# A chunked recurrence that takes all its heads through each step together

## The chip, the cores and the metric

The kernel runs on one core of a Trainium2 chip, as one launch. The metric is the time of one execution on the device in microseconds (us), shorter being better. A core has a matrix engine (TensorE: PE in the profile, with PEld for its weight loads), a vector engine (DVE), a scalar engine (ACT), GpSimd (POOL) and SyncE (SP), which here issues most of the DMAs. Each engine works through its own instructions in their order. Matrix results land in PSUM, from where DVE or ACT carries them to SBUF.

## The reference

Two layers over 2048 tokens of width 1024, 16 heads of 64. Layer 0 is RWKV-7 time mixing, layer 1 a dilated sliding-window attention. This document is about layer 0, whose recurrence is, per head and token:

```python
def step(state, inp):
    r_t, w_t, k_t, v_t, a_t, b_t = inp
    sa = jnp.einsum('bhvk,bhk->bhv', state, a_t)
    state = (state * w_t[:, :, None, :]
             + sa[..., None] * b_t[:, :, None, :]
             + v_t[..., None] * k_t[:, :, None, :])
    return state, jnp.einsum('bhvk,bhk->bhv', state, r_t)
...
y = _wkv7_scan(r, decay, k, v, -kk, kk * a)
y = ((y - mu) * lax.rsqrt(var + GN_EPS)).reshape(B, S, D) * ln_g + ln_b
bonus = jnp.sum(r * k * r_k, axis=-1, keepdims=True) * v
y = (y + bonus.reshape(B, S, D)) * jax.nn.silu(g)
return y @ w_out
```

## The kernel before

`phase1` makes the projections, `phase2` runs the recurrence and the output projection of layer 0, `phase3` is layer 1. All arithmetic is float32; a large matmul is three matmuls of split halves (`mm3`, L72 to L74).

In `phase2` the 2048 tokens are 32 chunks of 64. The state is carried from chunk to chunk, so each chunk depends on the one ahead of it. A chunk's work has these parts:

- **Loads** (`loads`, L844 to L866, on SP): the receptance and removal keys `ls1`, the keys `bk`, inverted blocks `tf`, corrections `ut` and the values in `x`, for the next chunk. `ls1`, `tf` and `ut` have two buffers, `bk` has one.
- **Preparation** (`prep`, L869 to L915) of the next chunk, which needs no state: products of keys (L881, tile `z`, 8 matmuls for each half of the heads), masked or copied out of PSUM by ACT (`ot`, L885) and DVE (L886, L888), small 32x32 products (L894, L903), and transposes of the keys (L910), which are the last to read `bk`.
- **The chain** (`chain`, L930 to L981), in three dependent steps. Step 1 multiplies the state `x` by the removal keys into `ps` (L942) and by the receptance into `y` (L944); `evac` copies the first half of `ps` to `qc` on ACT and the second on DVE, one behind the other. Step 2 applies the inverted blocks (L959), and the result is copied over the state's rows in `x` (L927 on ACT, then L928 on DVE). Step 3 makes the next state's update in `ps` (L965) and the rest of the output in `y` (L967); DVE scales it (`up`, L973) and adds the decayed state `xp` (L976), which POOL made from `x` in step 1 (L955).
- **The rest of the layer**, one chunk or more behind: group norm (`group_norm`, on DVE, ACT and POOL), transposes of the finished output (`finish`, L1024) and the output projection (`out_proj`, matmuls into `pd`, 128x128 weights); in the first chunks also the tail of phase 1's gate projection.

The heads are taken in two halves, `a` (heads of blocks 0 to 3) and `b` (blocks 4 to 7). Each half has its own pass through the three steps, half `b` about half a chunk behind half `a`, and its last step stands in the next chunk's turn (`behind`). Each turn of a half is followed by a slot, in which every other part gets one step:

```python
a, b = (chain(ch, hb, ls, yc) for hb in range(2))
for i, g in enumerate((a, behind, a, behind, a, b, a, b, a, b)):
    next(g, None)
    ...
    slot(i, ch)
```

That is the order in which the program records the work; the framework's scheduler then moves instructions on each engine by its own timeline. It is held by a few ties: an output projection's matmuls may not stand ahead of the chain's mark `LAG` steps back (`spread`, with `marks`), and some DVE work not ahead of the copy `DLAG` copies back (`yielding`, with `dmarks`).

Of the kernel before, what the change touches and what calls it, by code (L numbers as in the profile page):

```python
# [37 lines left out]
RATE = (2.4, 2.05)  # L38
# [10 lines left out]
class Trunk:  # L49
# [747 lines left out]
    def phase2(self, keep):  # L797
        tc, nc, ap = self.tc, self.nc, self.ap
        mm = nc.tensor.matmul
# [3 lines left out]
        with ExitStack() as ctx:  # L803
            def pool(name, bufs, ctx=ctx, **kw):
                return ctx.enter_context(tc.tile_pool(name=name, bufs=bufs, **kw))
            cctx = ExitStack()
            np_, xp, yp, zp, sp = pool("np", 1, keep), pool("xp", 3, keep), pool("yp", 2, keep), pool("zp", 3, keep), pool("sp", 4, keep)
            gp, tp = pool("gp", 2, keep), pool("tp", 2, keep)
            pz = pool("pz", 2, keep, space=PSUM)
            self.kept = dict(xp=xp, yp=yp, zp=zp, gp=gp, tp=tp, pz=pz)  # L810
            bp, ep, lp, kp = pool("bp", 1, cctx), pool("ep", 1, cctx), pool("lp", 2, cctx), pool("kp", 1, cctx)
            pc, py = pool("pc", 2, cctx, space=PSUM), pool("py", 2, cctx, space=PSUM)
            late = {}

# [4 lines left out]
            rows = (slice(0, 64), slice(64, 128))  # L819
            ls1, tf, ut = [], [], []  # L820
            for i in range(2):
# [5 lines left out]
                for s in range(2):  # L827
                    pmark = nc.gpsimd.memset(t[64 * s + 32:64 * s + 64, :, 0:32], 0.0)
# [97 lines left out]
            def evac(dst, src):  # L926
                nc.scalar.activation(dst[0], src[0], AF.Copy)  # L927
                dmarks.append(nc.vector.tensor_copy(dst[1], src[1]))  # L928

            def chain(ch, hb, ls2, yc):  # L930
                nonlocal pmark
                b, xt = ch % 2, X[ch]
                h = slice(4 * hb, 4 * hb + 4)
                hd = [(s, 4 * hb + j) for j in range(4) for s in range(2)]
                if ch == 0:
                    for s in range(2):
                        nc.vector.memset(xt[rows[s], s, h], 0.0)
                ps = pc.tile([P, 2, 4, 64], F32, name="ps")
                y = py.tile([P, 4, 64], F32, name="y")
                first = [None, None]  # L940
                for s, j in hd:
                    mm(ps[rows[s], 0, j - 4 * hb], ls1[b][:, s, j, 0], xt[:, s, j], start=True, stop=True)  # L942
                for s, j in hd:
                    i = mm(y[rows[s], j - 4 * hb], ls1[b][:, s, j, 1], xt[:, s, j], start=first[s] is None,  # L944
                           stop=False, skip_group_check=True)
# [5 lines left out]
                xp_ = kp.tile([P, 4, 64], F32, name="xp%d" % hb)  # L951
                pc_ = self.pch[:, ch // 4, ch % 4, h].unsqueeze(2).to_broadcast([P, 4, 64])
# [5 lines left out]
                for s, j in hd:  # L958
                    i = mm(ps[rows[s], 1, j - 4 * hb], tf[b][rows[s], j], qc[rows[s], j - 4 * hb], start=True, stop=True)  # L959
                marks.append(i)  # L960
                evac([xt[rows[s], s, h] for s in range(2)], [ps[rows[s], 1] for s in range(2)])
                yield
                if ch < NCH - 1:
                    for s, j in hd:
                        mm(ps[rows[s], 0, j - 4 * hb], ls2[:, s, j, 1], xt[:, s, j], start=True, stop=True)  # L965
                for s, j in hd:
                    i = mm(y[rows[s], j - 4 * hb], ls2[:, s, j, 0], xt[:, s, j], start=False, stop=True, skip_group_check=True)  # L967
                marks.append(i)
                if ch < NCH - 1:
                    nxt = [X[ch + 1][rows[s], s, h] for s in range(2)]  # L970
                    if ch:
                        up_ = kp.tile([P, 4, 64], F32, name="up")
                        nc.vector.tensor_tensor(up_, ps[:, 0], pc_, op=ALU.mult)  # L973
                    for s in range(2):
                        if ch:
                            nc.vector.tensor_tensor(nxt[s], up_[rows[s]], xp_[rows[s]], op=ALU.add)  # L976
                        else:
                            nc.vector.tensor_tensor(nxt[s], ps[rows[s], 0], pc_[rows[s]], op=ALU.mult)
                yield
                nc.scalar.activation(yc[:, h], y, AF.Copy)  # L980
                yield  # L981

            def group_norm(ch, yc, zc):
# [138 lines left out]
            for _ in prep(0, bks, ls2):  # L1122
                pass
            idle = iter(())
            gn, pre, behind = idle, idle, idle
            zs = []

            def slot(i, ch):
                nonlocal tail
                next(pre, None)  # L1130
                next(gn, None)
                next(elim, None)
                now[0] += 1
                if tail:
                    for _ in range(TAIL[i % 2]):
                        if tail and next(tail, 1) == 1:
                            tail = None
                fill(1, front)
                fill(2 if len(work) > 1 and ch >= RUSH else 1)
# [8 lines left out]
            for ch in range(NCH):  # L1148
                ls = ls2
                pre = idle  # L1150
                if ch + 1 < NCH:
                    bks = loads(ch + 1)
                    ls2 = lp.tile([P, 2, KC, 2, 64], F32, name="ls2")
                    pre = prep(ch + 1, bks, ls2)
                yc = yp.tile([P, KC, 64], F32, name="yc")
                a, b = (chain(ch, hb, ls, yc) for hb in range(2))
                for i, g in enumerate((a, behind, a, behind, a, b, a, b, a, b)):
                    next(g, None)
                    if i == 3 and ch:
# [6 lines left out]
                behind, ylast = b, yc  # L1166
            for _ in behind:
                pass
# [649 lines left out]
```

## Time and profile before

| | |
|---|---|
| median of 3 runs | 3888.3 us (3877.28 to 3890.25) |
| profiled execution | 3889.0 us |
| its span on the core | 3887.1 us |
| the recurrence: first matmul of step 1 to last of step 3 | 1086.4 to 1839.0 us, 752.6 us |
| one chunk, 752.6 / 32 | 23.5 us |
| TensorE busy in the whole span | 3700.6 us, 95% |

The profile is of one execution. Its own time is 0.7 us above the median. Starts are in us from the span's start. A row's busy time on PE runs from a matmul's start to its modelled end, and matmuls overlap, so the pace of matmuls is read from the distance of starts. A float32 matmul of the recurrence leaves two records in the trace: "x16" there is 8 matmuls. The transposes (L910, L1024) and the projections' split matmuls leave one each. The granted clock of PE (PEclk) is 1.0 at 2.4 GHz and 0.5 at 1.2 GHz.

### The profile page before, as it was taken

To read this page: it belongs to the slowest core of one execution; us is meant where nothing else is said; L and a number is where in the kernel's file an instruction comes from. 1 tells how busy PE (TensorE), PEld (TensorE's weight loads), DVE (VectorE), ACT (ScalarE), POOL (GpSimd) and SP (SyncE) were. 2 spreads that over 40 slices of the span, in tenths; PEclk is the share of its full clock that TensorE was granted. 3 is DMA by queue.
4 is the path that set the end of the run, shared out by engine and by line. 5 is a ranking of instruction groups with operands and counts; after the bars stand their busy time and mean duration, and the time that the engine had idled before them with its cause. 6 is when DMAs were issued, how large, how long until landed. Compare 5 with 4: busy or idle time off the path is not lost.

```text
span 3887.1 us, 79932 instructions
## 1 busy us (share of the span) xinstructions
PE 3700.6 (95%) x29328; PEld 2930.5 (75%) x29328; DVE 2494.7 (64%) x6213; ACT 1822.1 (47%) x4734; POOL 1430.8 (37%) x1377
## 2 busy tenths in 40 slices
PE   7899999999989999999898999999999999999999
PEld 5565667767777888888776877777777788887888
DVE  4884477889866565465576347777876664455556
ACT  4554443343334443344444233456666665565441
POOL 3341355564344343333344234533432220023232
PEclk9899999999979998899999999999999999999999
DMA  9774467675665443343578455665655565456655
GB/s 279 224 242 138 131 181 205 175 211 163 175 134 124 99 111 90 89 109 92 135 124 167 138 160 79 118 144 144 183 149 136 134 171 138 148 168 193 188 165 174
DMA packets 1027128, 595.31 MB, mean 153 GB/s; under 512 B 564912, under 2 KB 918576, under 8 KB 1020592
## 3 DMA queue, kind: packets, MB, share of 16 engines
q1 hardware_dynamic: 629040, 500.00, 46.1%
q10 hardware_dynamic: 397696, 90.20, 11.1%
q8 instruction: 232, 3.80, 0.4%
q14 instruction: 160, 1.31, 0.1%
HBM read 391.84 MB, written 198.18 MB: 152 GB/s over the span
## 4 chain that ended last, share of the span: by engine, by line
PE 69%; DVE 12%; DMA 7%; issue 4%; POOL 4%; ACT 2%; SPq 1%; ACTq 0%; DVEq 0%; POOLq 0%
PE ps L72 12%; PE ps L74 11%; PE ps L73 11%; PE sc L1640 4%; PE z L881 4%; PE pv L1672 4%; PE z L1661 3%; PE pd L72 2%; PE pd L73 2%; DVE q L1215 2%; PE pd L74 1%; POOL rr_st L1207 1%; DMA bk<-bkD 1%; PE z L269 1%; PE ps L942 1%
## 5 line engine op out<-in xcount | busy, mean ns | idle before, releaser
L1652 ACT ACTIVATE yt<-yt,nm 128x256 f32<-128x256 f32 (+1 forms) x768 | 345.1, 450 | 294.6 <-DVE nm L1648 293.8
L72 PE MATMUL ps<-xh,wh 128*128 128x512 f32 (+1 forms) x1248 | 449.7, 369 | 7.2 <-ACT xh L358 5.6
L73 PE MATMUL ps<-xl,wh 128*128 128x512 f32 (+1 forms) x1248 | 448.0, 360 | 5.4 <-DVE xl L360 4.0
L74 PE MATMUL ps<-xh,wl 128*128 128x512 f32 (+1 forms) x1248 | 445.1, 358 | 0.0
L72 PE MATMUL ps<-xh 128*128 128x512 f32 (+1 forms) x1152 | 419.1, 364 | 4.3 <-ACT ov L1485 2.8
L74 PE MATMUL ps<-xh,xl 128*128 128x512 f32 (+1 forms) x1152 | 400.4, 348 | 0.0
L73 PE MATMUL ps<-xl,xh 128*128 128x512 f32 (+1 forms) x1152 | 398.5, 346 | 0.0
L1207 POOL TENSOR_TENSOR rr_st<-rr_st,mh 128x8 f32<-128x8 f32 x128 | 215.6, 1684 | 469.6 <-DVE rr_st L1206 411.4
L74 PE MATMUL ps<-wh,xl 128*128 128x512 f32 x896 | 362.8, 407 | 14.4 <-DVE xl L66 13.8
L72 PE MATMUL ps<-wh,xh 128*128 128x512 f32 x896 | 370.8, 415 | 4.8 <-ACT q L1450 1.7
L73 PE MATMUL ps<-wl,xh 128*128 128x512 f32 x896 | 361.2, 403 | 0.7 <-DVE wl L1286 0.6
L72 PEld LDWEIGHTS ps<-xh,wh 128*128 128x128 f32 x1248 | 238.9, 193 | 81.3 <-issue 35.8
L1645 DVE CUSTOM_DVE_ANT_0 yt<-sc,amask 128x256 f32<-128x256 f32 (+1 forms) x768 | 237.2, 360 | 86.6 <-PE sc L1640 80.5
L73 PEld LDWEIGHTS ps<-xl,wh 128*128 128x128 f32 x1248 | 240.3, 193 | 60.7 <-issue 18.2
L74 PEld LDWEIGHTS ps<-xh,wl 128*128 128x128 f32 x1248 | 240.4, 193 | 51.6 <-issue 22.2
L72 PEld LDWEIGHTS ps<-xh 128*128 128x128 f32 x1152 | 218.0, 189 | 50.9 <-issue 19.0
L74 PEld LDWEIGHTS ps<-xh,xl 128*128 128x128 f32 x1152 | 217.8, 189 | 27.7 <-issue 0.3
L73 PEld LDWEIGHTS ps<-xl,xh 128*128 128x128 f32 x1152 | 218.5, 190 | 23.0 <-issue 0.3
L1212 POOL TENSOR_TENSOR rr_a<-rr_sq,TCS 128x512 f32<-128x512 f32 x128 | 183.4, 1433 | 114.4 <-DVE rr_sq L1210 98.0
L278 DVE SCALAR_TENSOR_TENSOR t<-hx,vecs,t 128x512 f32<-128x512 f32 x192 | 170.5, 908 | 81.9 <-ACT t L277 81.6
L1215 DVE TENSOR_TENSOR q<-rr_sq,TCS 128x256 f32<-128x256 f32 x256 | 219.7, 898 | 2.6
L74 PEld LDWEIGHTS ps<-wh,xl 128*128 128x128 f32 x896 | 172.0, 192 | 63.9 <-DVE xl L66 26.3
(341 smaller groups left out, 8830.7 us busy)
## 6 DMA issues: line engine op xcount, KB each, us to landing
hx<-hT SPq DMA_DIRECT2D x152, 256.5 KB
xb<-xbT SPq DMA_DIRECT2D x256, 128.0 KB
x<-Q SPq DMA_DIRECT2D x96, 256.0 KB
kq<-K SPq DMA_DIRECT2D x72, 256.0 KB
st<-in_w_in SPq DMA_DIRECT2D x64, 256.0 KB
arD<-ar SPq DMA_DIRECT2D x32, 512.0 KB
bkD<-bk SPq DMA_DIRECT2D x32, 512.0 KB
ls<-arD SPq DMA_DIRECT2D x64, 256.0 KB
```

The lines of the kernel that those rows point to most:

```text
L72: i = mm(out, lh, rh, start=first, stop=False, **kw)
L73: mm(out, lh, rl, start=False, stop=False, **kw)
L74: mm(out, ll, rh, start=False, stop=last, **kw)
L278: nc.vector.scalar_tensor_tensor(t1, hx[:, 0:512], self.vec["a_mix_mu"][:, m:m + 1], t1, op0=ALU.mult, op1=ALU.add)
L881: mm(at[s][:, j], bk[rows[s], 4 * hb + j].rearrange("p a t -> p (a t)"), ls1[b][rows[s], s, 4 * hb + j].rearrange("p a t -> p (a t)"), sta ...
L1207: nc.gpsimd.tensor_tensor(st[:, 1], st[:, 0], mh, op=ALU.pow)
L1212: nc.gpsimd.tensor_tensor(a, sq, TC[:, tt, None, :].to_broadcast([P, 8, 64]), op=ALU.mult)
L1215: nc.vector.tensor_tensor(v[:, :, lo:lo + 32], sq[:, :, hi:hi + 32], TS[:, tt, None, lo:lo + 32].to_broadcast([P, 8, 32]), op=ALU.mult)
L1640: j = mm(sc[h][:, x, :u.n * P], qt[r, c], kq[r, k1 - u.n * P:k1], start=True, stop=True)
L1645: nc.vector.tensor_tensor_reduce(out=u.pr[:, h, :nk], in0=sc[h][:, x, :nk], in1=amask[:, int(g == 0), 256 - nk:256], scale=1.0, scalar=-3e ...
L1652: nc.scalar.activation(u.pr[:, h, :nk], u.pr[:, h, :nk], AF.Exp, bias=nm[:, x, h:h + 1], accum_out=lm[:, x, h, 0:1])
L1672: prev[0] = self.after(mm(pv[e, u.i], u.vt[:, u.i + 2 - u.n + kb, e], u.pts[:, h, kb], start=(kb == 0), stop=(kb == u.n - 1)), prev[0])
```

## The change

Each step now takes all 16 heads at once, 16 matmuls of each kind where there were twice 8, into a whole PSUM bank `ps` that is taken anew for every step. The copies and updates that follow a step are as many as they were for one half, each twice as wide. The second half's pass, and with it `behind`, is gone: a chunk has four turns, followed by 3, 3, 3 and 1 slots (`SLOTS`), ten slots as before. Since the marks are half as many, `LAG` goes from 3 to 2 and `DLAG` from 4 to 2. The keys `bk` get a second buffer. The tail of the gate projection advances in slots 0 and 2 of each turn, 7 times in a chunk where it was 5. Line numbers behind the constants move by one or two.

```diff
-LAG = 3
-DLAG = 4
+LAG = 2
+DLAG = 2
...
+SLOTS = (3, 3, 3, 1)
...
-            bp, ep, lp, kp = pool("bp", 1, cctx), pool("ep", 1, cctx), pool("lp", 2, cctx), pool("kp", 1, cctx)
+            bp, ep, lp, kp = pool("bp", 2, cctx), pool("ep", 1, cctx), pool("lp", 2, cctx), pool("kp", 1, cctx)
...
-            def chain(ch, hb, ls2, yc):
+            def chain(ch, ls2, yc):
...
-                h = slice(4 * hb, 4 * hb + 4)
-                hd = [(s, 4 * hb + j) for j in range(4) for s in range(2)]
+                hd = [(s, j) for j in range(KC) for s in range(2)]
...
-                ps = pc.tile([P, 2, 4, 64], F32, name="ps")
-                y = py.tile([P, 4, 64], F32, name="y")
+                bank = lambda: pc.tile([P, KC, 64], F32, name="ps")
+                ps, y = bank(), py.tile([P, KC, 64], F32, name="y")
                 first = [None, None]
                 for s, j in hd:
-                    mm(ps[rows[s], 0, j - 4 * hb], ls1[b][:, s, j, 0], xt[:, s, j], start=True, stop=True)
+                    mm(ps[rows[s], j], ls1[b][:, s, j, 0], xt[:, s, j], start=True, stop=True)
...
-                qc = kp.tile([P, 4, 64], F32, name="qc%d" % hb)
-                evac([qc[:, 0:2], qc[:, 2:4]], [ps[:, 0, 0:2], ps[:, 0, 2:4]])
+                qc = kp.tile([P, KC, 64], F32, name="qc")
+                evac([qc[:, 0:4], qc[:, 4:8]], [ps[:, 0:4], ps[:, 4:8]])
...
-                        pmark = nc.gpsimd.tensor_tensor(xp_[rows[s]], xt[rows[s], s, h], pc_[rows[s]], op=ALU.mult)
-                yield
-                yield
+                        pmark = nc.gpsimd.tensor_tensor(xp_[rows[s]], xt[rows[s], s], pc_[rows[s]], op=ALU.mult)
+                yield
+                ps = bank()
...
-                evac([xt[rows[s], s, h] for s in range(2)], [ps[rows[s], 1] for s in range(2)])
-                yield
+                evac([xt[rows[s], s] for s in range(2)], [ps[rows[s]] for s in range(2)])
+                yield
+                ps = bank()
...
-                        up_ = kp.tile([P, 4, 64], F32, name="up")
-                        nc.vector.tensor_tensor(up_, ps[:, 0], pc_, op=ALU.mult)
+                        up_ = kp.tile([P, KC, 64], F32, name="up")
+                        nc.vector.tensor_tensor(up_, ps, pc_, op=ALU.mult)
...
-                a, b = (chain(ch, hb, ls, yc) for hb in range(2))
-                for i, g in enumerate((a, behind, a, behind, a, b, a, b, a, b)):
-                    next(g, None)
-                    if i == 3 and ch:
+                steps = chain(ch, ls, yc)
+                for i, n in enumerate(SLOTS):
+                    next(steps)
+                    if i == 0 and ch:
                         for _ in gn:
                             pass
                         gn = normed(ch - 1, ylast)
-                    slot(i, ch)
+                    for k in range(n):
+                        slot(k, ch)
```

On every engine the order of the program is the same before and after from its start up to the recurrence, and again from early in `phase3` to the end. What moves on PE is seen in a chunk's turn. First the tenth chunk (chunk 9) of the kernel before. L910 is the last reader of a chunk's keys, L881 the first reader of the next chunk's; L942, L944 are step 1, L959 step 2, L965, L967 step 3.

```order
L910 MATMUL z<-cst,bk 128x64 x8
L942 MATMUL ps<-x,ls_1_10362 64x64 x6
L944 MATMUL y<-x,ls_1_10362 64x64 x8
L965 MATMUL ps<-x,ls_12665 64x64 x8
L967 MATMUL y<-x,ls_12665 64x64 x8
L1093 MATMUL pd<-ones,acc 128x2 x2
L959 MATMUL ps<-qc_13366,tf_10366 64x64 x8
L881 MATMUL z<-ls_0_10355,bk 128x128 x4
L942 MATMUL ps<-x,ls_1_10362 64x64
L944 MATMUL y<-x,ls_1_10362 64x64
L942 MATMUL ps<-x,ls_1_10362 64x64 x7
L881 MATMUL z<-ls_0_10355,bk 128x128 x4
```

Steps of the two halves stand behind each other, in pieces of 1 to 8, and between the last reader of `bk` and the first reader of the next `bk` there are 40 matmuls. Now the changed kernel on PE, the beginning of chunk 16, where L943 and L945 are step 1 and L882 the preparation's first products:

```order
L943 MATMUL ps<-x,ls_0_10355 64x64 x16
L945 MATMUL y<-x,ls_0_10355 64x64 x16
L882 MATMUL z<-ls_1_10362,bk 128x128 x8
L73 MATMUL pd<-yh,wh 128x256
L74 MATMUL pd<-yl,wh 128x256
```

and the end of the same chunk, where L967 and L969 are step 3, L895 and L904 the 32x32 products and L911 the transposes of the keys:

```order
L895 MATMUL z<-ut_10365,ot_15526 32x32 x8
L895 MATMUL z<-ut_10365,ot_15573 32x32 x8
L967 MATMUL ps<-x,ls_15154 64x64 x16
L969 MATMUL y<-x,ls_15154 64x64 x7
L904 MATMUL z<-tf_10366,t 32x32 x16
L969 MATMUL y<-x,ls_15154 64x64 x9
L911 MATMUL z<-cst,bk 128x64 x8
```

A step stands in runs of 16, and of the preparation's products 8 stand together. Within such a run of 8 the matmuls alternate between the upper and the lower 64 rows of the array in 19 of the 26 cases; before, runs of 4 on one half of the rows are the rule. Counted over the whole recurrence, from the first matmul of step 1 to the last of step 3, PE's matmuls stand in these runs of one kind:

| kind | matmuls | runs before | runs after |
|---|---|---|---|
| steps 1 and 3 (128 rows, 64 columns) | 2032 | 238 | 147 |
| step 2 (64x64) | 512 | 104 | 66 |
| key products (L881) | 500 | 121 | 100 |
| 32x32 products, key transposes, finishing transposes, sums | 1668 | 174 | 174 |
| projections into `pd` | 1385 before, 1368 after | 206 | 143 |

On DVE, in the kernel before, step 1's copy to `qc` (L928) stands ahead of a chunk's norm statistics (L986), since the two halves take turns:

```order
L928 COPY x<-ps 64x256
L1081 SCALAR_TENSOR_TENSOR t_16539<-pd,hgate,t_16539 128x256
L928 COPY qc_16624<-ps 128x128
L973 TENSOR_TENSOR up<-ps,pch 128x256
L976 TENSOR_TENSOR x<-up,xp_16463 64x256 x2
L986 BN_STATS st<-yc 128x6 x4
```

In the changed kernel the whole state is updated (L975, L978), and then the statistics (L988) and other work stand ahead of the next chunk's copy (L929). Here the chunk is one of those that finish a block of two chunks (L1031) at that place:

```order
L975 TENSOR_TENSOR up<-ps,pch 128x512
L978 TENSOR_TENSOR x<-up,xp 64x512 x2
L988 BN_STATS st<-yc 128x6 x7
L1083 SCALAR_TENSOR_TENSOR t_15625<-pd,hgate,t_15625 128x256
L988 BN_STATS st<-yc 128x6
L1067 TENSOR_TENSOR yl<-yt,yh 128x4x128
L992 TENSOR_TENSOR mv<-st 128x8
L993 TENSOR_TENSOR mv<-st 128x8
L994 TENSOR_TENSOR mv<-st 128x8
L1031 SCALAR_TENSOR_TENSOR yt<-z,vecs,sg 128x128 x4
L995 TENSOR_TENSOR mv<-mv 128x8
L929 COPY qc<-ps 128x256
```

Between the update of the state and the copy there is now the work of one group norm and of the finishing, where there was none.

## Rows read from the trace of the kernel before

**Rows 1.** The page's head: the span, and busy time by engine with its share of the span and its instructions.

```profile
span 3887.1 us, 79932 instructions
PE 3700.6 (95%) x29328; PEld 2930.5 (75%) x29328; DVE 2494.7 (64%) x6213; ACT 1822.1 (47%) x4734; POOL 1430.8 (37%) x1377
```

**Rows 2.** The table by stretch: the whole recurrence, and four of the twelve stretches in it at the lower clock. Columns: length, busy us (instructions) of PE, PEld, DVE, ACT and POOL, granted clock, share and rate of DMA.

```profile
core 0: us, PE busy (x) PEld busy (x) DVE busy (x) ACT busy (x) POOL busy (x), PEclk, DMA share, GB/s
1086.40:1839.00 752.60, 719.84 (x10178) 627.86 (x10177) 438.04 (x1336) 312.32 (x860) 291.20 (x328) 0.91 0.45 103
...
1125.50:1142.60 17.10, 16.43 (x151) 14.23 (x153) 7.57 (x21) 2.82 (x8) 1.22 (x2) 0.50 0.28 74
...
1306.40:1320.00 13.60, 13.60 (x125) 11.44 (x125) 6.32 (x23) 5.22 (x15) 3.97 (x4) 0.50 0.34 70
1466.80:1480.50 13.70, 13.70 (x101) 12.22 (x101) 5.03 (x15) 4.53 (x14) 2.60 (x3) 0.50 0.35 86
...
1589.70:1610.20 20.50, 20.50 (x198) 17.75 (x198) 9.26 (x34) 6.04 (x18) 7.25 (x8) 0.50 0.26 58
```

**Rows 3.** Waits of PE within the recurrence, longest in total first: waiting line, releaser, us in total, times, longest.

```profile
PE z L881 <- DMA bk<-bkD: 16.1, 13, 2.2
PE z L881 <- issue: 10.9, 7, 2.7
```

**Rows 4.** The timeline of PE in chunk 9: start us, us, line, tiles, records; in brackets the idle time of PE ahead of it.

```profile
1298.08 0.71 PE L910 MATMUL z<-cst,bk 64*128 64x64 f32 x8
...
1301.16 0.68 PE L959 MATMUL ps<-qc,tf 64*64 64x64 f32 x16
1303.95 1.13 PE L881 MATMUL z<-ls,bk 64*128 64x128 f32 x8 [2.11 <-DMA bk<-bkD]
```

**Rows 5.** The timeline of PE at the full clock, near the end of the recurrence; same columns.

```profile
1804.29 1.16 PE L881 MATMUL z<-ls,bk 64*128 64x128 f32 x8
1805.37 0.45 PE L959 MATMUL ps<-qc,tf 64*64 64x64 f32 x8
...
1806.83 0.33 PE L959 MATMUL ps<-qc,tf 64*64 64x64 f32 x2
1807.09 0.39 PE L72 MATMUL pd<-yh,xh 128*128 128x256 f32 x1
...
1827.59 0.39 PE L72 MATMUL pd<-yh,wh 128*128 128x256 f32 x1
...
1828.50 0.69 PE L942 MATMUL ps<-x,ls 128*64 128x64 f32 x16
1829.02 0.64 PE L944 MATMUL y<-x,ls 128*64 128x64 f32 x16
1829.58 0.39 PE L72 MATMUL pd<-yh,wh 128*128 128x256 f32 x1
...
1831.11 0.39 PE L72 MATMUL pd<-yh,wh 128*128 128x256 f32 x1
...
1833.45 0.68 PE L959 MATMUL ps<-qc,tf 64*64 64x64 f32 x16
1834.07 0.39 PE L72 MATMUL pd<-yh,wh 128*128 128x256 f32 x1
```

**Rows 6.** The timeline of PE at one of the few places of the kernel before where key products of both halves of the rows alternate; same columns.

```profile
1112.10 1.17 PE L881 MATMUL z<-ls,bk 64*128 64x128 f32 x16
1113.20 0.69 PE L942 MATMUL ps<-x,ls 128*64 128x64 f32 x16
```

**Rows 7.** The timeline of PE inside a stretch at the lower clock; same columns.

```profile
1470.46 2.07 PE L881 MATMUL z<-ls,bk 64*128 64x128 f32 x8
1472.46 0.90 PE L944 MATMUL y<-x,ls 128*64 128x64 f32 x10
1473.29 0.58 PE L72 MATMUL pd<-yh,wh 128*128 128x256 f32 x1
...
1474.87 0.48 PE L965 MATMUL ps<-x,ls 128*64 128x64 f32 x2
```

**Rows 8.** The timeline of PE: two long waits for keys, and one of the shorter ones; same columns.

```profile
1464.57 1.13 PE L881 MATMUL z<-ls,bk 64*128 64x128 f32 x8 [2.40 <-issue]
...
1589.40 1.77 PE L881 MATMUL z<-ls,bk 64*128 64x128 f32 x8 [2.23 <-DMA bk<-bkD]
...
1640.67 1.13 PE L881 MATMUL z<-ls,bk 64*128 64x128 f32 x8 [1.48 <-issue]
```

**Rows 9.** Groups of instructions in the recurrence, by line and shape: busy us in total, mean ns of one, idle time ahead of them and what ended it.

```profile
L986 DVE BATCH_NORM_STATS2 st<-yc 128x6 f32<-128x64 f32 x252 | 38.3, 212 | 7.0 <-ACT yc L980 6.0
L1029 DVE SCALAR_TENSOR_TENSOR yt<-z,vecs,sg 128x128 f32<-128x128 f32 x120 | 33.6, 342 | 19.2 <-PE z L1024 19.1
L1081 DVE SCALAR_TENSOR_TENSOR t<-pd,hgate,t 128x256 f32<-128x256 f32 x54 | 25.9, 479 | 46.0 <-PE pd L74 44.7 <-DMA bk<-bkD 0.9
L973 DVE TENSOR_TENSOR up<-ps,pch 128x256 f32<-128x256 f32 x60 | 25.2, 419 | 47.5 <-PE ps L965 47.3
...
L1065 DVE TENSOR_TENSOR yl<-yt,yh 128x512 fp32r<-128x512 f32 x28 | 19.7, 720 | 0.8 <-ACT yh L1064 0.4
...
L913 ACT ACTIVATE ls<-z 128x512 f32<-128x512 f32 x64 | 38.2, 597 | 25.1 <-PE z L910 24.0
...
L1000 POOL TENSOR_TENSOR zc<-x,beta 64x512 f32<-64x512 f32 x64 | 67.7, 1057 | 10.0 <-issue 3.5 <-PE z L1024 1.9
```

More of the change, by code (lines that the diff above doesn't have):

```diff
@@ L928, in evac @@
                 dmarks.append(nc.vector.tensor_copy(dst[1], src[1]))
-            def chain(ch, hb, ls2, yc):
+            def chain(ch, ls2, yc):
                 nonlocal pmark
                 b, xt = ch % 2, X[ch]
-                h = slice(4 * hb, 4 * hb + 4)
-                hd = [(s, 4 * hb + j) for j in range(4) for s in range(2)]
+                hd = [(s, j) for j in range(KC) for s in range(2)]
                 if ch == 0:
                     for s in range(2):
-                        nc.vector.memset(xt[rows[s], s, h], 0.0)
-                ps = pc.tile([P, 2, 4, 64], F32, name="ps")
-                y = py.tile([P, 4, 64], F32, name="y")
+                        nc.vector.memset(xt[rows[s], s], 0.0)
+                bank = lambda: pc.tile([P, KC, 64], F32, name="ps")
+                ps, y = bank(), py.tile([P, KC, 64], F32, name="y")
                 first = [None, None]
                 for s, j in hd:
-                    mm(ps[rows[s], 0, j - 4 * hb], ls1[b][:, s, j, 0], xt[:, s, j], start=True, stop=True)
+                    mm(ps[rows[s], j], ls1[b][:, s, j, 0], xt[:, s, j], start=True, stop=True)
                 for s, j in hd:
-                    i = mm(y[rows[s], j - 4 * hb], ls1[b][:, s, j, 1], xt[:, s, j], start=first[s] is None,
+                    i = mm(y[rows[s], j], ls1[b][:, s, j, 1], xt[:, s, j], start=first[s] is None,
                            stop=False, skip_group_check=True)
@@ L953, in chain @@
+                pc_ = self.pch[:, ch // 4, ch % 4].unsqueeze(2).to_broadcast([P, KC, 64])
                 if 0 < ch < NCH - 1:
                     for s in range(2):
-                        pmark = nc.gpsimd.tensor_tensor(xp_[rows[s]], xt[rows[s], s, h], pc_[rows[s]], op=ALU.mult)
+                        pmark = nc.gpsimd.tensor_tensor(xp_[rows[s]], xt[rows[s], s], pc_[rows[s]], op=ALU.mult)
                 yield
-                yield
-                for s, j in hd:
-                    i = mm(ps[rows[s], 1, j - 4 * hb], tf[b][rows[s], j], qc[rows[s], j - 4 * hb], start=True, stop=True)
@@ L960, in chain @@
-                marks.append(i)
-                evac([xt[rows[s], s, h] for s in range(2)], [ps[rows[s], 1] for s in range(2)])
-                yield
+                ps = bank()
+                for s, j in hd:
+                    i = mm(ps[rows[s], j], tf[b][rows[s], j], qc[rows[s], j], start=True, stop=True)
+                marks.append(i)
+                evac([xt[rows[s], s] for s in range(2)], [ps[rows[s]] for s in range(2)])
+                yield
+                ps = bank()
                 if ch < NCH - 1:
@@ L964, in chain @@
                     for s, j in hd:
-                        mm(ps[rows[s], 0, j - 4 * hb], ls2[:, s, j, 1], xt[:, s, j], start=True, stop=True)
+                        mm(ps[rows[s], j], ls2[:, s, j, 1], xt[:, s, j], start=True, stop=True)
                 for s, j in hd:
-                    i = mm(y[rows[s], j - 4 * hb], ls2[:, s, j, 0], xt[:, s, j], start=False, stop=True, skip_group_check=True)
+                    i = mm(y[rows[s], j], ls2[:, s, j, 0], xt[:, s, j], start=False, stop=True, skip_group_check=True)
@@ L968, in chain @@
                 marks.append(i)
                 if ch < NCH - 1:
-                    nxt = [X[ch + 1][rows[s], s, h] for s in range(2)]
+                    nxt = [X[ch + 1][rows[s], s] for s in range(2)]
                     if ch:
-                        up_ = kp.tile([P, 4, 64], F32, name="up")
-                        nc.vector.tensor_tensor(up_, ps[:, 0], pc_, op=ALU.mult)
+                        up_ = kp.tile([P, KC, 64], F32, name="up")
+                        nc.vector.tensor_tensor(up_, ps, pc_, op=ALU.mult)
@@ L977, in chain @@
                         else:
-                            nc.vector.tensor_tensor(nxt[s], ps[rows[s], 0], pc_[rows[s]], op=ALU.mult)
+                            nc.vector.tensor_tensor(nxt[s], ps[rows[s]], pc_[rows[s]], op=ALU.mult)
                 yield
-                nc.scalar.activation(yc[:, h], y, AF.Copy)
+                nc.scalar.activation(yc, y, AF.Copy)
                 yield
@@ L1124, in phase2 @@
             idle = iter(())
-            gn, pre, behind = idle, idle, idle
+            gn, pre = idle, idle
             zs = []
@@ L1162, in phase2 @@
                         gn = normed(ch - 1, ylast)
-                    slot(i, ch)
+                    for k in range(n):
+                        slot(k, ch)
                 for _ in pre:
                     pass
-                behind, ylast = b, yc
-            for _ in behind:
-                pass
+                ylast = yc
             cctx.close()
```

3 lines of the change are left out of this document (1 added, 2 removed).

## The prediction

> **What bounds the kernel now.** TensorE is busy for 95% of the span [rows 1], and so it is in the stretch that the change touches. The table by stretch gives the recurrence 752.6 us, of which PE is busy for 719.8; DVE has 438, ACT 312 and POOL 291 [rows 2]. So 32.8 us are idle time of PE, and the question is what the 719.8 hold. The reader should look at three things.
>
> First, the waits of PE. Two lines make up nearly all the idle time: 16.1 + 10.9 = 27.0 us in 20 waits stand ahead of L881, the first matmuls on a new chunk's keys [rows 3]. "issue" in the second means that the profile shows no releaser. The timeline of chunk 9 shows what happens [rows 4]: the last reader of the old keys (L910) starts at 1298.08, the load may go out then, and the first reader of the new keys starts at 1303.95, after 2.11 us of idle time; the 40 matmuls between them did not last as long as the load.
>
> Second, the price of a run. At the full clock, one matmul of step 2 alone takes 1807.09 - 1806.83 = 0.26 us to the next kind of matmul, 8 in a row take 1834.07 - 1833.45 = 0.62. So each matmul costs 0.05 and each run 0.21. Steps 1 and 3: 16 matmuls from 1828.50 to 1829.58, 1.08. Projections: 6 in 0.91 (1827.59 to 1828.50), 18 in 2.34 (1831.11 to 1833.45), so 0.12 each and again 0.2 for the run. Key products: 4 in 1.08 [rows 5]. A change of kind costs about 0.2 us, whatever the kinds, and 843 runs cost 843 x 0.2 = 169 us of 752.6.
>
> Third, the clock. Its mean over the recurrence is 0.91 [rows 2]: 18% of the time, 135 us in twelve stretches (the first runs on from before the recurrence), ran at 1.2 GHz and the rest at 2.4. There the same runs take 2.00 for 1.08 (4 key products) and 1.58 for 0.91 (6 projections) [rows 5, 7], 1.8 times as long. So the lower clock costs 135 x (1 - 1/1.8) = 60 us. Seven of the waits for keys last about 2 us or more, and behind each of the seven the clock falls within 2.5 us: three of them start PE again at 1303.95, 1464.57 and 1589.40 [rows 4, 8], and the stretches behind them begin at 1306.4, 1466.8 and 1589.7; the one from 1125.5 begins inside the longest wait, 2.7 [rows 2, 3]. Behind shorter ones the clock falls in some cases; behind the 1.48 at 1640.67 [rows 8] it does not.
>
> **The change, part by part.** The matmuls are the same in number and shape.
>
> *Runs.* By the table of runs, steps 1 and 3 lose 238 - 147 = 91 runs, step 2 38, the projections 63: 192 x 0.2 = 38.4 us. The 17 projection matmuls that now stand behind the last step are neither lost nor gained. The price of a run is read at many places and is steady; I bound this term by 30 and 42.
>
> *Alternating key products.* In 19 runs of 8, matmuls on the lower and the upper 64 rows alternate. The one clean case in the trace has 8 such matmuls from 1112.10 to 1113.20, 1.10 us [rows 6], as long as 4 on one side. Each of the 19 saves 2 x 1.08 - 1.10 = 1.06, together 20 us. The bounds are 0 (if that case were peculiar) and 20; I take 20, since both halves of the keys are there long before.
>
> *The second key buffer.* The load for the next chunk now waits for the last reader of the buffer before last. Counting PE's work in the order, at the prices above, between that reader and the first use: 2 to 5 us before, 13 to 25 us after. In chunk 9 the load took all of 5.9 us from the last reader's start to the first use [rows 4], so 13 are enough, and the 27.0 us go. SP's queue is the same in kind: the loads of `tf` and `ut`, which stand ahead of the keys there, wait for readers of the chunk before last. Bounds: 20 (something else is late then) and 27; I take 27.
>
> *The clock.* If the waits go, what follows them goes. The seven stretches behind the long waits sum to 99 us, so 99 x 0.444 = 44 us. Against that I set one new stretch of their mean length, 14 us, cost 6: net 38. Bounds: 0 and 55.
>
> The Trainium skill, page TensorE: Matmul & The Clock Gate, section "A second HAM failure mode: psum-queue depth-cycling", tells of a kernel whose short idles between groups of matmuls, from cycling through PSUM banks, were enough to make the clock swing. By it the falls would come from the changes of kind, which remain 629, and the new bank for each step would add to them; the clock's 38 us would be 0 and the sum 3810. The rows put the falls behind the waits, which no group change of 0.2 us resembles, so the rule stands as a rival.
>
> *New waits.* With one pass instead of two, PE needs other work while a step's result is copied. The copies are twice as wide: on DVE 0.42 for 256 columns [rows 9], so 0.84 for 512; on ACT 0.60 for 512 (L913). Behind step 2 that is 0.60 + 0.84 = 1.44, behind step 3 three DVE instructions, 2.5 us. PE's work between steps, counted from the order at the prices above, is 2.0 to 5.3 us behind step 1, 2.0 to 5.3 behind step 2, and 1.9 to 6.9 behind step 3, mostly 4.5 to 6. So they are covered but for the tightest. The tightest in the steady part is the DVE place shown: ahead of the copy to `qc` stand 8 statistics (38.3 / 252 = 0.15 each), one L1081 (0.48), one L1065 (0.72), four L1029 (0.34 each) and four small ones on 8 columns, which I estimate at 0.3 each: 1.2 + 0.5 + 0.7 + 1.4 + 1.2 = 5.0 [rows 9], and the copy itself, 0.4. PE offers 2.4 (step 1 with what stands within it) and 2.0 behind it. So 1.0 us is missing, in one chunk of four from the sixth on: 7 us. Bounds: 0 and 40 (a good us in each chunk).
>
> *Fewer, wider instructions* on DVE, ACT and POOL save fixed costs on engines that wait for PE anyway; nothing. The gate's tail, 7 steps a chunk for 5, and the marks only move projections within the recurrence; their runs are counted above. What hides the rest of `phase3` does not move, since its order is the same.
>
> The sum, against the profiled execution: 3889.0 - 38.4 - 20 - 27 - 38 + 7 = 3772.6; I say **3772 us**. That execution is 0.7 us above the median of the runs shown, which I leave in. The recurrence would take 636 us, 19.9 a chunk, and 3% of the whole is far more than the 0.3% that a measurement of this kernel can tell from no change.
>
> **Rivals.**
>
> *The clock is no better* (0.17). The many small matmuls themselves hold the clock down, and the falls only happened to begin at waits. For it: five of the twelve stretches are behind no long wait, and a stretch lasts up to 20.5 us with PE busy throughout [rows 2]. Against it: the seven of seven. Time: 3772 + 38 = 3810.
>
> *The chain shows* (0.14). DVE's and ACT's queues hold a step's copies up by a good us in every chunk, as no second half covers it: +33 us, and a stretch or two at the lower clock: about 3815. For it: the DVE rows of the changed order; against it: in the kernel before, waits other than for keys were 32.8 - 27.0 = 5.8 us in all, in an order made by the same scheduler, with gaps between steps as small as 1.9.
>
> *Better still* (0.14). No stall of 1 us and no new fall, and one or two of the other stretches go: 3772 - 7 - 6 - 15 = 3744.
>
> *Slower than before* (0.03). POOL makes `xp` from `x`, now 2 x 1.06 us (L1000 has that shape [rows 9]), and step 2's copy overwrites that `x`, so it waits for POOL, whose queue holds the norm's product and the squares' sum ahead of it. PE's work is 752.6 - 27 - 58 - 38 = 630 us, 19.7 a chunk against 23.5 now, so it decides from 3.8 us of waiting in every chunk; at 5 us it gives 3772 + 160 - 7 = 3925. Against it: PE reaches the end of step 2 at least 5 us behind the new state.
>
> *The grouping gives nothing* (0.04): a run of 16 hides no change of kind, only keys and clock gain: 3889 - 27 - 38 = 3824.
>
> **How the numbers follow.** My forecast has 0.48, by itself 3755 to 3790. The range 3738 to 3820 leaves out 0.03 for the slow case, part of the case without grouping and the tails of the others, about 0.15. All but the slow case, and a small part next to it, are faster by more than 11.7 us (0.3%): 0.95 faster, 0.02 the same, 0.03 slower.
>
> **What would show it.** In the changed profile: no wait of PE ahead of L882 for `bk`; in the timeline, step 1 as 32 + 32 records in about 1.96 us to the next kind; L882 as 16 records in 1.1 us; a granted clock of 0.95 or more over the recurrence, and a recurrence of some 636 us; waits of PE ahead of L960 (step 2) from DVE `qc`, about 1 us in every fourth chunk. I am wrong if the clock stays near 0.91, if 8 alternating key products take 2.2 us, or if PE waits for DVE or ACT by more than 20 us in all.

## The result, and the profile after

The changed kernel takes 3769.8 us (median of 4, 3765.4 to 3778.4) beside 3889.3 for the kernel before (3877.3 to 3902.5): a ratio of 0.967, with an interval of 0.964 to 0.970. The forecast was 3772. The profile is of the slowest of the four executions.

The page's head of the changed kernel, and the table by stretch: the recurrence, and two of the stretches at the lower clock in its steady part.

```profile
span 3776.5 us, 79506 instructions
PE 3604.4 (95%) x29328; PEld 2863.5 (76%) x29328; DVE 2481.2 (66%) x6055; ACT 1809.5 (48%) x4638; POOL 1437.8 (38%) x1317
```

```profile
core 0: us, PE busy (x) PEld busy (x) DVE busy (x) ACT busy (x) POOL busy (x), PEclk, DMA share, GB/s
1093.00:1723.00 630.00, 618.59 (x10160) 555.16 (x10160) 431.82 (x1173) 298.79 (x761) 280.56 (x267) 0.97 0.55 123
...
1426.60:1430.00 3.40, 3.40 (x19) 3.40 (x17) 1.25 (x3) 0.39 (x1) 0.00 (x0) 0.50 0.69 123
1597.30:1600.70 3.40, 3.40 (x29) 2.83 (x26) 1.46 (x7) 2.80 (x9) 0.95 (x2) 0.50 1.11 223
```

PE is busy for 95% of the span, as before [rows 1]; the share shows nothing of the change. The recurrence does: 630.0 us for 752.6 [rows 2], 19.7 a chunk, with idle time of PE down from 32.8 to 11.4 us and the granted clock up from 0.91 to 0.97. The lower clock holds for some 44 us in place of 138 (135 in the prediction, from the rounded mean). The recurrence lost 122.6 us; in this one execution it also began 6.6 us later, behind work that the change does not touch, so the spans differ by less.

The waits of PE in the recurrence of the changed kernel, longest in total first (waiting line, releaser, us, times, longest):

```profile
PE z L904 <- ACT t L900: 3.1, 2, 2.9
PE z L895 <- issue: 2.0, 1, 2.0
PE z L882 <- DVE ls L889: 1.6, 5, 0.3
PE z L882 <- issue: 1.4, 1, 1.4
```

The 20 waits for keys [rows 3] are gone; `bk` is named nowhere. What is left lies in the first six chunks, but for five waits of 0.3 us ahead of L882 and one of 0.25 ahead of L904. The timeline of PE in a steady chunk (start, us, line, tiles, records, idle time ahead):

```profile
1495.71 1.15 PE L943 MATMUL ps<-x,ls 128*64 128x64 f32 x32
1496.69 1.10 PE L945 MATMUL y<-x,ls 128*64 128x64 f32 x32
1497.72 1.16 PE L882 MATMUL z<-ls,bk 64*128 64x128 f32 x16
1498.81 0.39 PE L73 MATMUL pd<-yh,wh 128*128 128x256 f32 x1
...
1502.38 1.13 PE L882 MATMUL z<-ls,bk 64*128 64x128 f32 x8 [0.31 <-DVE ls L889]
```

Step 1 of all heads is one run of 32 + 32 records in 2.01 us, where a half took 16 + 16 in 1.08 [rows 5]; 8 alternating key products take 1.09 us, as in [rows 6].

### The profile page after: what moved, and what is told of

The parts are those of the page before. It is cut to its first block, busy times and chain, and to the rows that moved or that the text cites. A ratio compares the mean times of both kernels' runs of the same rounds, so it can differ in the third digit from the quotient of the medians.

```text
span 3776.5 us, 79506 instructions
## 1 busy us (share of the span) xinstructions
PE 3604.4 (95%) x29328; PEld 2863.5 (76%) x29328; DVE 2481.2 (66%) x6055; ACT 1809.5 (48%) x4638; POOL 1437.8 (38%) x1317
## 5 line engine op out<-in xcount | busy, mean ns | idle before, releaser
L73 PEld LDWEIGHTS ps<-wh,xh 128*128 128x128 f32 x896 | 171.3, 191 | 58.3 <-ACT xh L66 11.1
L1216 DVE TENSOR_TENSOR q<-rr_sq,TCS 128x256 f32<-128x256 f32 x256 | 211.0, 865 | 2.7
```

The costliest lines, as they stand in the source:

```text
L73: i = mm(out, lh, rh, start=first, stop=False, **kw)
L1216: nc.vector.tensor_tensor(v[:, :, lo:lo + 32], sq[:, :, hi:hi + 32], TS[:, tt, None, lo:lo + 32].to_broadcast([P, 8, 32]), op=ALU.mult)
```

## The experiments

Two kernels take the change apart, two change only the order of the key products, one of them a second time without the grouping, one deals PSUM out otherwise, one puts the old ties back, and two make PE stall by hand. To compare them, every run of matmuls of one kind in a recurrence is priced as in the prediction, at the full clock [rows 5] and at the lower one [rows 7]. "At full clock" is the sum of the prices, "lower clock" what the stretches at 1.2 GHz add, "beyond" the rest: the idle time of PE (32.8 us before, 11.4 in the changed kernel), and what the prices miss. "Changes" counts the runs of one kind in the order of the instructions. The last column leaves out the first eight chunks or so, where the gate's tail still runs.

| kernel | time, us | ratio (95%) | changes | recurrence | at full clock | lower clock | beyond | us at 1.2 GHz, from 1250 us to its end |
|---|---|---|---|---|---|---|---|---|
| before | 3889.3 | | 843 | 752.7 | 647 | 59 | 47 | 85 |
| changed | 3769.8 | 0.967 (0.964 to 0.970) | 630 | 630.1 | 590 | 17 | 23 | 14 |
| e1: second key buffer alone | 3768.0 | 0.969 (0.965 to 0.973) | 737 | 635.2 | 588 | 26 | 22 | 0 |
| e2: grouping alone | 3857.1 | 0.991 (0.988 to 0.994) | 703 | 727.1 | 617 | 55 | 55 | 65 |
| e3: changed, alternation forced | 3780.7 | 0.973 (0.969 to 0.977) | 670 | 642.2 | 577 | 28 | 37 | 14 |
| e4: changed, one side, then the other | 3786.1 | 0.974 (0.971 to 0.978) | 649 | 651.9 | 603 | 26 | 23 | 7 |
| e5: changed, PSUM dealt otherwise | 3733.7 | 0.958 (0.955 to 0.961) | 670 | 603.7 | 539 | 25 | 40 | 3 |
| e6: e1, one side, then the other | 3787.4 | 0.972 (0.968 to 0.976) | 698 | 662.4 | 605 | 29 | 29 | 0 |
| e7: changed, ties as before | 3776.0 | 0.969 (0.966 to 0.972) | 629 | 638.0 | 585 | 20 | 33 | 0 |
| e8: changed, short stalls by hand | 3785.7 (one execution) | | 634 | 651.2 | 589 | 27 | 36 | 31 |
| e9: changed, long stalls by hand | 3832.9 (one execution) | | 611 | 688.1 | 585 | 40 | 64 | 92 |

Times were measured in three sessions, in which the kernel before took 3889.3 (changed), 3887.5 (e1 to e4) and 3896.9 us (e5 to e8), and in a fourth 3903.8 in a single execution (e9); so ratios are what compares across rows. By the medians alone the changed kernel, e1 and e7 all stand at 0.969.

**The key buffer alone.**

```diff
-            bp, ep, lp, kp = pool("bp", 1, cctx), ...
+            bp, ep, lp, kp = pool("bp", 2, cctx), ...
```

> The kernel before with two buffers for a chunk's keys and nothing else changed: the two halves of the heads still take turns. The order of the instructions changes a little by itself, since step work need no longer stand behind the keys: the matmuls of the recurrence fall into 737 runs of one kind where the kernel before has 843, and 40 of the runs of 8 key products alternate between lower and upper rows. At the prices of the prediction (about 0.2 us a run, 1.1 us for 8 alternating key products) the order alone is worth 53 us. Theory A (the stalls for keys and the falls of the clock behind them are one thing, and a second buffer ends both): 53 + 27 for the waits + some 38 for the clock, so about 3770, nearly the whole of the change, and a granted clock of 0.95 or more over the recurrence. Theory B (the changes of kind hold the clock down, and only the grouping takes them away): 53 + 27, clock near 0.91 to 0.92, about 3809.

3768.0 us: theory A to within 2 us. The stretch of its recurrence, and the waits of PE in it, longest first:

```profile
1089.90:1725.10 635.20, 625.73 (x10182) 550.41 (x10181) 448.79 (x1335) 311.17 (x859) 302.26 (x328) 0.95 0.52 123
```

```profile
PE z L1024 <- DVE mv L993: 3.0, 6, 0.5
PE z L1024 <- DVE ls L888: 2.1, 1, 2.1
```

One edit of one number does as much as the whole change. From 1250 us on there is no microsecond at the lower clock, with two halves taking turns and 737 changes of kind:

```profile
1250.00:1725.10 475.10, 472.12 (x8035) 422.04 (x8030) 342.22 (x1024) 238.02 (x666) 236.08 (x248) 1.00 0.51 119
```

And the order, which nobody wrote anew, got cheaper by 59 us: 106 runs less, and 48 groups of 8 key products in one piece at the full clock, of which 40 alternate and take 1.09 us (7 more take 1.64). The kernel before has one such group of 1.10.

**The grouping alone.**

```diff
-            bp, ep, lp, kp = pool("bp", 2, cctx), ...
+            bp, ep, lp, kp = pool("bp", 1, cctx), ...
```

> The changed kernel with one buffer for a chunk's keys in place of two: all 16 heads go through each step together, but the next chunk's keys wait for the last reader of this chunk's. The order has 703 runs of one kind (before 843, changed kernel 630), and no run of key products alternates between lower and upper rows; by the prices of the prediction that is worth 29 us. Theory A (clock falls with the stalls for keys): the 16 or more stalls of 1 to 2.5 us ahead of the key products stay and so do the falls behind them: about 3860, clock near 0.91. Theory B (changes of kind hold the clock down): 29 + some 38 for the clock, about 3822, clock 0.95 or more though the stalls are there.

3857.1: theory A again. Its recurrence, its waits for keys, one of them, and the stretch behind that:

```profile
1084.70:1811.80 727.10, 686.52 (x10161) 610.55 (x10161) 426.07 (x1174) 299.57 (x762) 278.15 (x267) 0.91 0.48 106
```

```profile
PE z L882 <- DMA bk<-bkD: 24.1, 20, 5.5
PE z L882 <- issue: 7.0, 6, 2.8
```

```profile
1343.72 1.13 PE L882 MATMUL z<-ls,bk 64*128 64x128 f32 x8 [2.83 <-issue]
```

```profile
1345.30:1372.60 27.30, 27.30 (x228) 24.27 (x230) 8.81 (x29) 5.10 (x12) 6.53 (x6) 0.50 0.30 61
```

It has fewer changes of kind than e1 and the clock of the kernel before, 0.91. All seven of its waits of 1.9 us or more ahead of L882 (1.90 to 5.5, two of them put down to ACT by the profile) have a stretch at the lower clock that begins inside them or within 1.7 us of their end; ten more there, of 0.9 to 1.5 us, have none within 2.5 us, though three have one 2.9 to 3.9 us behind. The two parts alone are worth 120 us (e1) and 30 (e2), and both together 120: they do not add up.

**The key products' order.** e3 ties each of the 8 to the one recorded ahead of it (alternating sides); e4 does the same with the two loops exchanged (one side, then the other):

```diff
+                    prev = None
                     for j in range(4):
                         for s in range(2):
-                            mm(at[s][:, j], ...)
+                            prev = self.after(mm(at[s][:, j], ...), prev)
```

> The changed kernel, with the 8 key products of a half made to go first on the lower, then on the upper 64 rows, so that none alternate. 649 runs. Theory A (alternation is what shortens them): 21 us above the changed kernel, about 3791, and each 4 key products 1.08 us. Rival (the one case of 1.10 us for 8 in the kernel before was peculiar, and the alternation is worth nothing): 3770.

> The changed kernel, with the 8 key products of a half made to alternate between the lower and the upper 64 rows in every chunk (in the changed kernel only part of them do). 670 runs, 63 of 64 key-product groups alternating in 7 or all 8 of their matmuls. Theory A (the alternation itself makes 8 matmuls as short as 4): 22 us below the changed kernel, about 3748. Rival (the second of the two banks that they write comes free late, and the wait for it takes what is won): no gain, 3765 to 3775, with waits ahead of the key products from the readers of z.

e4 came out 16 us above the changed kernel for an expected 21, and its timeline shows why: 8 in one piece, one side behind the other, take not twice 1.08 but 1.63.

```profile
1507.51 1.71 PE L883 MATMUL z<-ls,bk 64*128 64x128 f32 x16
1509.14 0.39 PE L73 MATMUL pd<-yh,wh 128*128 128x256 f32 x1
```

e3 missed: 3780.7, not 3748, and not for its rival's reason either: the waits for readers of `z` ahead of the key products are 0.7 us in all. The tie made them alternate in sequence, not in one piece:

```profile
1500.48 0.48 PE L883 MATMUL z<-ls,bk 64*128 64x128 f32 x2
1500.89 0.33 PE L961 MATMUL ps<-qc,tf 64*64 64x64 f32 x2
1501.15 1.16 PE L883 MATMUL z<-ls,bk 64*128 64x128 f32 x14
1502.23 1.14 PE L961 MATMUL ps<-qc,tf 64*64 64x64 f32 x30
```

The first product stands alone in 56 of the 63 groups, 0.41 us, with other work between it and the seven (1.09). That leaves 13 us of gain at the full clock, and waits (+14) and the lower clock (+11) take more than that back.

**The same in halves.** e1 with e4's order of products.

> The kernel before with two buffers for the keys, as in the first experiment, but with the 8 key products of a half made to go first on one side and then on the other. 698 runs of one kind (that experiment has 737), 53 groups of 4 + 4 (1.64 us each, as measured with this order in the grouped kernel) where it had 48 alternating ones of 1.09. Theory (alternation is worth 0.55 us a group, and is why the second buffer alone does as much as the whole change): 48 x 0.55 = 26 more, 39 runs x 0.2 = 8 less, about 18 above the first experiment: 3785. Rival (alternation plays no part, the buffer alone does it by waits and clock): 3768 less 8 for the runs, 3760.

3787.4, 19 above e1 by the medians and 11 by the ratios, whose intervals overlap; the prices at the full clock go the same way, 605 for 588. So the alternation is very likely part of what the key buffer gives. The expectation took 48 groups of e1 for alternating where 40 are; with 40 its sum is 14 above e1, not 18. With no product alternating, grouped (e4, 0.974) and in halves (e6, 0.972), the kernels stand level again.

**One tile of two banks.** The steps' results and `y` get one bank each where they had two, and the two banks that come free are taken as one tile for the key products and the transposes:

```diff
-            pc, py = pool("pc", 2, cctx, space=PSUM), pool("py", 2, cctx, space=PSUM)
+            pc, py = pool("pc", 1, cctx, space=PSUM), pool("py", 1, cctx, space=PSUM)
+            pa = pool("pa", 1, cctx, space=PSUM)
-                    at = [pz.tile([P, 4, P], F32, name="z") for _ in range(2)]
+                    at = pa.tile([P, 2, 4, P], F32, name="za")
+                    at = [at[:, s] for s in range(2)]
-                tr = [pz.tile([P, KC, 64], F32, name="z") for _ in range(2)]
+                tr = pa.tile([P, 2, KC, 64], F32, name="za")
+                tr = [tr[:, s] for s in range(2)]
```

> The changed kernel with PSUM dealt out otherwise: one bank in place of two for the steps' results and one for y, and the two banks that come free taken together as one tile, which the 8 key products of a half (and the 16 transposes of the keys) write. No product can start before both its banks are free, so all 63 groups of key products alternate between lower and upper rows by the order alone, with none split into 1 + 7 as in the kernel that forced the alternation; 670 runs of one kind. Theory (what 1 + 7 lost there is the split: 0.4 us for the single product and a further run around it): 38 more alternating groups than the changed kernel has, at 0.55 to 1.06 us, less 40 runs at 0.2 us, so 13 to 32 us below it: 3738 to 3757. Rival (one bank where there were two makes PE wait for the copies out of it): the stalls grow from some 23 us in the changed kernel's recurrence to 40 or more, the clock falls behind them, and it stays at 3770 or above.

3733.7, ratio 0.958: faster than both kernels, with intervals that do not meet, and 4 us below the theory's range. That range left out the transposes, and took 25 groups of the changed kernel for alternating where 18 are. The recurrence, and the timeline of PE in one chunk:

```profile
1084.50:1688.20 603.70, 573.71 (x10171) 508.64 (x10171) 432.25 (x1173) 293.97 (x763) 279.65 (x266) 0.95 0.57 128
```

```profile
1494.16 0.71 PE L914 MATMUL za<-cst,bk 64*128 64x64 f32 x16
1494.81 0.33 PE L946 MATMUL ps<-x,ls 128*64 128x64 f32 x2
...
1497.70 1.16 PE L884 MATMUL za<-ls,bk 64*128 64x128 f32 x16
1498.79 0.66 PE L1029 MATMUL z<-cst,zc 128*128 128x128 f32 x4
1500.58 0.44 PE L963 MATMUL ps<-qc,tf 64*64 64x64 f32 x6 [1.14 <-DVE qc L932]
```

All key products take 1.09 us a group, and the 16 transposes of the keys, which now alternate too, 0.65, with a busy time of 0.71 that 8 of one side had in [rows 4]. The rival was right that waits grow, idle time of PE from 11.4 to 30.0 us, and wrong that they take the gain. What the missing second banks cost by themselves was not measured. The last row is the wait that the prediction expected in the changed kernel: 1.1 us from DVE `qc`, five times, four chunks apart.

**The ties.**

```diff
-LAG = 2
-DLAG = 2
+LAG = 3
+DLAG = 4
```

> The changed kernel with LAG and DLAG as in the kernel before (3 and 4 in place of 2 and 2). 629 runs of one kind, as the changed kernel (630). Theory (these numbers place the projections and were counted with the runs): no difference, 3766 to 3776. Rival (tighter marks are what lets the grouped steps go through): slower by 10 us or more, with waits ahead of the steps.

3776.0, a ratio of 0.969 for 0.967: no difference that can be measured, as the theory says.

**Stalls by hand.** In some chunks (here those of e9) behind the copy to `qc`:

```diff
+                for _ in range({9: 30, 13: 34, 17: 38, 21: 42, 25: 46}.get(ch, 0)):
+                    nc.vector.tensor_copy(qc[:, 4:8], qc[:, 4:8])
```

> The changed kernel with a stall put in by hand in six chunks of the steady part (9, 12, 15, 18, 21, 24), where the changed kernel has almost none: behind the copy of step 1's result DVE copies half of that tile onto itself 8, 11, 14, 17, 20 and 23 times, so step 2 comes 2 to 10 us later than it would, with PE's other work (2 to 5 us) to cover a part. No load is delayed by it, and the order keeps 634 runs of one kind. Theory A (any stall of PE of about 2 us or more brings the clock down, whatever PE waits for): behind each stall of 2 us or more ahead of step 2 the granted clock falls to 1.2 GHz within 2.5 us; the half-clock time in the recurrence grows by 10 us or so for each; time about 3800 to 3830. Theory B (the falls go with the loads of keys or the key products themselves, not with the stall): the stalls alone, no new half-clock stretches, about 3780 to 3800.

e8 did not decide. PE found other work, and its stalls stayed at 1.9 us and below. Of two new stretches at the lower clock one begins at 1598.1, 1.7 us behind the longest of them, the other (1519.6 to 1540.1) where PE had no wait ahead of it.

> The stall by hand once more, longer and in five chunks: 30, 34, 38, 42 and 46 copies of half of step 1's result onto itself in chunks 9, 13, 17, 21 and 25 (one such copy took 0.28 us with the others queued around it; alone some 0.2), so 6 to 10 us between step 1 and step 2 where PE has some 5 us of other work. In the run before it the stalls stayed at 1.0 to 1.9 us, and only the longest, 1.9, had a fall of the clock behind it. Theory A (a stall of PE of about 2 us or more brings the clock down, whatever PE waits for): five stalls of 2 us or more, each with a stretch at 1.2 GHz that begins inside it or within 2.5 us of its end; some 15 to 25 us of stalls and 5 x 6 for the clock, about 3815 to 3830. Theory B (the falls go with late keys, not with the stall): the stalls alone, 3785 to 3800, and no more stretches than the changed kernel has.

e9 did. The waits of PE from 1250 us on, one of the five places in the timeline, and the table of two of the five stretches:

```profile
PE ps L962 <- DVE qc L953: 18.6, 5, 6.4
PE z L895 <- DVE ls L889: 12.8, 5, 2.6
```

```profile
1374.18 1.07 PE L895 MATMUL z<-ut,ot 32*32 32x32 f32 x32 [2.55 <-DVE ls L889]
...
1384.45 1.12 PE L962 MATMUL ps<-qc,tf 64*64 64x64 f32 x16 [2.47 <-DVE qc L953]
```

```profile
1371.90:1389.00 17.10, 11.50 (x128) 10.92 (x129) 11.67 (x32) 4.55 (x11) 1.08 (x1) 0.50 0.31 68
1460.70:1477.70 17.00, 11.07 (x125) 10.40 (x126) 12.31 (x36) 4.04 (x10) 0.55 (x1) 0.50 0.29 64
```

In each of the five chunks DVE's queue, full of copies, holds up the small products of L895 by 2.6 us, and in each the clock falls inside that wait, 0.3 to 1.5 us after PE went idle (here PE was idle from 1371.6 to 1374.2, and the fall is at 1371.9). No key was late. So no late key is needed: with the copies, five chunks of five have a stretch of 14 to 21 us that begins there; in the changed kernel, without them, one of the five has one, of 3.4 us and at another place. Since the falls come early in the waits, what the work just ahead of them adds to the stall is not separated. The order of that kernel has 611 changes of kind, fewer than any other.

## Why the prediction was right

**What bounds the kernel, and the three shares.** The split of the table is the prediction's own sum, measured: at the full clock 647 to 590, that is -57 (forecast -38.4 for runs and -20 for alternation); lower clock 59 to 17, -42 (forecast -38); beyond 47 to 23, -24 (forecast -27 for the keys, +7 for new waits). Together -123 for a forecast of -116, and a recurrence of 630 us for 636.

**Runs and alternation.** The price of a change of kind held (step 1 in 2.01 us for 1.96). Of 26 groups in one piece, 18 took the 1.09 us that one case in the trace had promised (19 were counted), so the bound of 0 for that term can be dropped; e4 puts its worth in the changed kernel, by itself, at 16 us. Five of the other groups took 1.64, one side behind the other in one piece, which is 0.5 us less than two pieces and was not in the sum.

**What the sum did not ask is whose the 57 us are.** It took them for the grouping's, and gave the kernel without the grouping's effect 3824 us (the last rival). e1 has no grouping and stands at 3768. The step that was wrong is that rival's "only keys and clock gain": the order is made anew when a buffer is added, and in halves, with the second key buffer, it has 106 changes fewer and 40 alternating groups of 8. The grouping does save changes (737 to 630, 21 us), but it has only 18 such groups, and 22 fewer at 1.06 us give 23 us back. The total came out right since both parts were counted from the order of the whole change; a forecast of the key buffer alone by that reasoning is 56 us too high, and one of the grouping alone (3889 - 58 + 7 = 3838) 19 too low.

**Key waits.** Right: no wait for `bk` is left with two buffers, in either form (the changed kernel, e1), and 31 us of them with one (e2).

**The clock.** Right, and now shown, not only read off seven coincidences: stalls for keys away without the grouping, and the steady part has no time at the lower clock (e1); grouping without that, and it has 65 us (e2); stalls made by DVE alone, and 92 (e9). The alternation is not the reason: e6 has none of it, and no time at the lower clock from 1250 us on. These stretches are of one execution each, but the granted clock of the whole program, in every execution on record, agrees: 0.972 to 0.976 in the changed kernel and e1, 0.955 to 0.967 in the kernel before, 0.961 to 0.968 in e2. The rule of the Trainium skill, page TensorE: Matmul & The Clock Gate, section "A second HAM failure mode: psum-queue depth-cycling", which stood as a rival at 3810 us, would have tied the falls to the short pauses between groups: e1 with 737 changes of kind loses 26 us to the lower clock, e2 with 703 loses 55, so here they do not set it. That new stretches would come was allowed for, with 14 us; the steady part has 13.6, though in three pieces.

**New waits.** The place was right, the wait was not there. DVE's row of work ahead of the copy to `qc` in the tightest chunk:

```profile
1511.92 0.99 DVE L988 BATCH_NORM_STATS2 st<-yc 128x6 f32<-128x64 f32 x7 [0.36 <-ACT yc L982]
...
1516.47 0.41 DVE L929 COPY qc<-ps 128x256 f32<-128x256 f32 x1
```

From the first statistic to the end of the copy are 4.96 us, for 5.0 estimated with 0.4 more for the copy. But DVE begins 0.6 us ahead of step 1 (1512.54), and step 2 starts 4.85 us behind that (1517.39), not 4.4, so the copy is there 0.5 us early. The +7 should have been 2: five waits of 0.3 us, and those ahead of the key products, not of step 2. In e5, where the 1.1 us between are gone with the alternation, it appears at the size expected.

**The other rivals.** The chain showing in every chunk, POOL being late with `xp`: neither is among the waits of the changed kernel. "Better still" fails on the three new stretches and on the waits of the first chunks, which were not in the sum: 2.9, 2.0 and 1.4 us.

**Still open:** why the clock falls at 1426.6, 1597.3 and 1675.8 in the changed kernel, and at 1519.6 in e8, with PE at work on either side of the fall. The first three cost 6 us together (13.6 x 0.444, by the prediction's rate). Three of the four, all but 1426.6, share a place: PE had just begun the sums over a block (L1095, L1097 in e8), which come once in four chunks.

```profile
1596.23 0.33 PE L960 MATMUL ps<-qc,tf 64*64 64x64 f32 x2
1596.49 0.61 PE L1095 MATMUL pd<-ones,acc 128*128 128x2 f32 x4
```

Four more falls, in e3 (1362.3, 1519.3), e4 (1529.5) and e9 (1279.7), come 0.4 to 1.3 us behind the start of these sums. But in the changed kernel the sums at 1362.8, 1441.7 and 1519.1, with the same work right ahead of them, have no fall, nor have those of e1, e6 and e7; nothing was run to test it. And that the scheduler's model of a late key is what scattered the old order was seen in its result only; that was not tested either.

## What to carry to other kernels

Before redesigning a dependent chain, give the transfer that it waits for a second buffer and look at the order again: the same cause can sit behind the stall, the clock behind the stall, and a scattered order. Price parts of a change apart, each with the order that it would have by itself, since two edits can earn the same microseconds. Where matmuls use half the rows, let the halves alternate in one piece, and get that by giving both results one tile, not by tying the instructions to one another.

## What the runs showed of the hardware

- Eight float32 matmuls of 64 rows: 1.09 us alternating between the lower and the upper rows, 1.63 one side behind the other in one piece, 2 x 1.08 in two pieces. Sixteen transposes of 64 rows: 0.65 alternating, twice 0.64 by sides.
- The clock fell inside a wait of PE of 2.6 us in five cases out of five with nothing but DVE behind the wait, and stayed at 1.2 GHz for 14 to 21 us, in the two stretches shown with PE idle for a third of it (11.5 of 17.1 us busy). Shorter waits go both ways: in e2 ten of 0.9 to 1.5 us had no fall within 2.5 us of their end, while in the kernel before one of 1.02 us, which ended at 1491.70, had one 2.4 us behind it, at 1494.1.
